# New places for the first query tile's attention among the main products, and an earlier load of x's first rows

## The chip, the cores and the metric

The kernel runs on one core of one Trainium2 chip. The metric is the device time of one execution in microseconds, taken as the median of three runs: 1147.26 us (1147.25 to 1148.64). The profiled execution took 1147.47 us, of which 1145.7 us lie between its first and its last instruction.

## The reference

Two layers of a decoder trunk work on x of 512 tokens by 1024 features, all in float32. Each layer is a mixer and then a gated MLP, both between root-mean-square norms. What matters here is the mixer's differential attention with 4 heads, each of which has two score maps and subtracts the second, weighted, from the first:

```
proj = rms_norm(x, g) @ w_in                     # 1024 -> 2560 columns
for query block i of 128 rows, head h:
    s = q[h, 0:2] @ k[h, 0:2].T * scale          # causal: keys of the blocks 0..i
    p = softmax(s)
    a = p[0] - lam * p[1]
    o[h] = a @ v[h]                              # 128 x 128
o = rms_norm(o, subln_g) * (1 - lam_init)        # a norm over each head's 128 columns
mix = concat(o, retention, pooling) @ w_out
x = x + rms_norm(mix, g2);  then the MLP: up projection, short convolution, gelu gate, down projection
```

There are four query blocks (i = 0 to 3). The first one has 128 keys only.

## The kernel before, in words

**Main products.** Nearly all of the time goes into four large products of each layer: the input projection (five strips of 512 columns: s = 0 for q, 1 for k, 2 for v, 3 for retention's q, k, v, 4 for gates and pooling), the output projection, the MLP's up projection and its down projection. Each operand is split into a high and a low part, so that one product of a 128-row slice takes three matmuls (`mm3`, line 489). Weights come through SyncE's DMA queue into one of three `raw` buffers (`emit_dma`, line 261) and are split by ScalarE (line 300) and VectorE (line 301) into `wa` and `wb` (`emit_split`, line 270).

**The planner.** While Python emits the program it counts main products in `now`: 512 columns of one matmul are one unit. After each `mm3` it calls `serve` (line 366) with three more units. The small steps of the mixer are generators (`scores`, `turns`, `values`, `outputs`, lines 886 to 915), each of which yields the place of its next step, in units from the layer's start, and the names of the steps that must have been emitted before. `serve` emits the step with the smallest place among those that are due and whose needs are done, until none is left. Places come from the table `PLACE` (line 45); a place is thus a due time, rounded up to the next multiple of three. `in_order` (line 332) ties every TensorE instruction behind the one emitted before it, so TensorE runs exactly in the planner's order, and if an instruction waits, everything behind it waits too. The order on VectorE and ScalarE is chosen by the framework from priorities; the planner's steps are emitted `ahead` of the main products' own work.

The planner counts 96 units for each of the five strips of the input projection. The four generators of attention are registered once strip 1 is emitted (line 977), at 192 units, and attention of the first query tile runs beside strip 2.

**The steps of one query tile i.** For each head h:

- `unit_a(h, i, m)` (line 720), m = 0 and 1: two score matmuls into a bank of role "s". There are two such banks, used in turn. VectorE adds the mask (line 730) and takes the maximum (line 731), ScalarE takes the exponential (line 733) and reads its row sum. After m = 1 VectorE forms the difference of the two maps (lines 738 to 740).
- `unit_b(h, i)` (line 742): TensorE turns the probabilities, ScalarE copies them out (line 749).
- `unit_c(h, i)` (line 752): TensorE multiplies them with v into the bank "o", 128 columns for each head. After the last head (h = 3) follows the norm: four squares with row sums on ScalarE (line 766), an addition (line 767), a reciprocal root of ten small VectorE instructions (lines 394 to 402), and one product of 512 columns (line 770) that leaves the normed tile in SBUF.
- `unit_e(i)` (line 781), once for each query tile: TensorE turns the four heads of the normed tile; it needs line 770's result. The result is split into the output projection's operand (lines 778 and 779).

Needs that matter: the scores of the fourth head need the first head's turning (`(l, "b", n - 3)`, line 889); a turning needs the values of two heads before it (line 897).

**The opening.** Before layer 0, x transposed (`xt`, four parts of 512 KB, each with two of the eight 128-feature slices) goes through two buffers into the split operand `ht` (`load_xt`, `split_xt`, lines 535 and 539); a third part waits until a buffer has been split. x itself (four tiles of 128 rows, `load_x`, line 567) is loaded as well, since the rows' norm factors (`row_factors`, line 447) come from it. They are squares on ScalarE (line 451) and a reciprocal root on VectorE. The factors are needed when the first strip's results leave PSUM (line 642). All of these transfers, the constants, the parameters and the four lambda vectors (line 249) are issued from SyncE's queue, in the order in which the code stands in lines 555 to 588. ScalarE's exponential for lambda is line 255.

Of the kernel before, what the change touches and what calls it, by code (L numbers as in the profile page):

```python
# [54 lines left out]
    ],  # L55
    "b": [[234, 235, 232, 242], [275, 278, 280, 287], [326, 334, 338, 320], [381, 385, 388, 418]],
    "c": [[241, 236, 242, 243], [282, 260, 284, 296], [330, 342, 326, 350], [386, 402, 397, 427]],
    "e": [264, 317, 373, 452],
    "rows": 404,
    "r1": [395, 431, 465, 513],  # L60
# [77 lines left out]
def tile_trunk(ctx: ExitStack, tc: tile.TileContext, x, xt, win, wout, wup, wdown, gpost, par, lam, const, out):  # L138
# [44 lines left out]
    def t4():  # L183
        return t4p.tile([P, D], F32, tag="t4", name=nm("t4"))
# [85 lines left out]
    def emit_split():  # L270

        j = state["split"]
        if j >= NU:
            return False
        kind, l, i = units[j][1]
        if i >= LAST3.get(kind, NFF):
            if not state["space"]:
                return False
            h, lo = state["space"].pop(0)
        else:  # L280
            if state["free"] == 0:
                return False
            state["free"] -= 1
            k = state["slot"] = (state["slot"] + 1) % NW
            h, lo = (wp.tile([P, D], F32R, tag=f"w{n}{k}", name=nm("w" + n)) for n in "ab")
        state["split"] += 1
        r = raws.pop(j)
        if kind == "down":
            se.copy(h, r)  # L289
            ve.tensor_tensor(out=lo, in0=r, in1=h.bitcast(F32), op=ALU.subtract)  # L290
        else:
            pr = params[l]
            if kind == "out":
                cuts = [(h, lo, r, pr["ws"][:, i:i + 1])]
            else:

                g = pr["gmix" if kind == "in" else "gmlp"]
                cuts = [(x[:, 0:512], x[:, 512:D], r[:, c * 512:(c + 1) * 512], g[:, 2 * i + c:2 * i + c + 1]) for c, x in enumerate((h, lo))]
            for a, b, x, sc in cuts:
                se.activation(a, x, AF.Copy, scale=sc)  # L300
                low = ve.scalar_tensor_tensor(b, x, sc, a.bitcast(F32), op0=ALU.mult, op1=ALU.subtract)  # L301
                if j == 0:
                    after(low, 0)
        halves[j] = [h, lo] if kind in LAST3 else [(x[:, 0:512], x[:, 512:D]) for x in (h, lo)]
        emit_dma()
        return True
# [228 lines left out]
    def load_xt(j):  # L535
        xparts[j] = t4()
        sy.dma_start(xparts[j], xt[j])

    def split_xt(j):
        r = xparts.pop(j)  # L540
        for c in range(2):
            dh = hth[:, 2 * j + c, :]
            if j or c:
                se.copy(dh, r[:, c * S:(c + 1) * S])
            else:
                opened.append(ve.tensor_copy(dh, r[:, c * S:(c + 1) * S]))
            low = ve.tensor_tensor(out=htl[:, 2 * j + c, :], in0=r[:, c * S:(c + 1) * S], in1=dh.bitcast(F32), op=ALU.subtract)
            if not (j or c):
                opened.append(low)
# [17 lines left out]
    def load_x(t):  # L567
        sy.dma_start(xs[:, t, :], x[t * P:(t + 1) * P, :])
        done.add((0, "xT", t))

    split_xt(0)
    emit_split()
    load_xt(2)
    split_xt(1)
    load_xt(3)
    load_x(0)
    emit_split()
    sy.dma_start(cst[:, 0:NCONST], const)
    derive_params(0)
# [618 lines left out]
```

## Time and profile before

| what | us |
|---|---|
| median of three runs | 1147.26 |
| the profiled execution | 1147.47 |
| its span, first to last instruction | 1145.7 |
| TensorE matmuls busy | 1133.6 (99%) |
| TensorE weight loads busy | 944.3 (82%) |
| VectorE busy | 738.8 (64%) |
| ScalarE busy | 548.1 (48%) |
| GpSimd busy | 11.9 (1%) |

Matmuls are pipelined in the records: a matmul of 512 columns is shown as busy for 0.39 us, while in a dense stretch the next one starts 0.23 us later. So the busy share of TensorE doesn't tell what is lost; one reads the distances between the starts. A row such as "L338 PE MATMUL ps_m<-wa,ht ... x3" is three matmuls in a row that write the tile ps_m from wa and ht. In the mixer ps_m is a main product of the strips 1 to 4, ps_s a score, ps_b a turning, ps_o the values. PE is TensorE, ACT ScalarE, DVE VectorE, SPq the queue of SyncE.

### The profile page before, as it was taken

To read this page: it belongs to the slowest core of one execution; us is meant where nothing else is said; L and a number is where in the kernel's file an instruction comes from. 1 tells how busy PE (TensorE), PEld (TensorE's weight loads), DVE (VectorE), ACT (ScalarE), POOL (GpSimd) and SP (SyncE) were. 2 spreads that over 40 slices of the span, in tenths; PEclk is the share of its full clock that TensorE was granted. 3 is DMA by queue.
4 is the path that set the end of the run, shared out by engine and by line. 5 is a ranking of instruction groups with operands and counts; after the bars stand their busy time and mean duration, and the time that the engine had idled before them with its cause. 6 is when DMAs were issued, how large, how long until landed. Compare 5 with 4: busy or idle time off the path is not lost.

```text
span 1145.7 us, 14829 instructions
## 1 busy us (share of the span) xinstructions
PE 1133.6 (99%) x5474; PEld 944.3 (82%) x5474; DVE 738.8 (64%) x1667; ACT 548.1 (48%) x1051; POOL 11.9 (1%) x20
## 2 busy tenths in 40 slices
PE   9999999999999999999999999999999999999997
PEld 6788878988888888888888888789888888888886
DVE  6988696777556457423777896876856655663224
ACT  6965543565444345312367754454645434452221
POOL 1000000000000000000000000000000000000000
PEclk9999999999999999999999999999999999999999
DMA  8411131332222232224023111313323232323211
GB/s 326 137 65 57 57 114 39 111 129 92 105 98 85 100 107 95 101 92 147 1 96 125 56 54 53 114 38 114 125 97 106 79 107 100 103 76 109 95 50 58
DMA packets 31320, 109.22 MB, mean 95 GB/s; under 512 B 3728, under 2 KB 4240, under 8 KB 31248
## 3 DMA queue, kind: packets, MB, share of 16 engines
q1 hardware_dynamic: 29808, 105.11, 26.5%
q10 hardware_dynamic: 1440, 3.17, 0.8%
q8 instruction: 43, 0.70, 0.2%
q14 instruction: 29, 0.24, 0.1%
HBM read 106.16 MB, written 2.10 MB: 94 GB/s over the span
## 4 chain that ended last, share of the span: by engine, by line
PE 91%; DVE 4%; ACT 2%; DMA 2%; issue 1%; SPq 0%; DVEq 0%; ACTq 0%
PE ps L338 72%; PE ps_m L338 11%; PE ps_b L341 2%; PE ps_b L338 2%; PE ps_o L338 2%; PE ps_s L338 1%; PE ps L341 1%; DMA rt<-in_lam 1%; DMA raw<-in_wout 1%; DVE ks L670 1%; DMA raw<-in_win 1%; ACT wa L300 0%; ACT t L733 0%; DVE space L301 0%; DVE wb L301 0%
## 5 line engine op out<-in xcount | busy, mean ns | idle before, releaser
L338 PE MATMUL ps<-ht,wb 128*128 128x512 f32 (+1 forms) x1176 | 305.0, 368 | 0.0
L338 PE MATMUL ps<-ht,wa 128*128 128x512 f32 (+1 forms) x1176 | 304.8, 367 | 0.0
L338 PEld LDWEIGHTS ps<-ht,wa 128*128 128x128 f32 x1176 | 210.3, 189 | 36.5
L338 PEld LDWEIGHTS ps<-ht,wb 128*128 128x128 f32 x1176 | 210.1, 188 | 36.5
L301 DVE SCALAR_TENSOR_TENSOR wa<-raw,par,wa 128x512 fp32r<-128x512 f32 x128 | 95.8, 749 | 143.5 <-ACT wa L300 143.2
L300 ACT ACTIVATE wa<-raw,par 128x512 fp32r<-128x512 f32 x128 | 92.2, 721 | 185.6 <-PE ps L338 173.4
L338 PE MATMUL ps<-wa,c 128*128 128x512 f32 x448 | 126.3, 394 | 0.0
L290 DVE TENSOR_TENSOR wb<-raw,wa 128x1024 fp32r<-128x1024 f32 x38 | 46.5, 1225 | 82.1 <-ACT wa L289 82.1
L301 DVE SCALAR_TENSOR_TENSOR wb<-raw,par,wb 128x512 fp32r<-128x512 f32 x128 | 95.8, 748 | 4.3 <-ACT wb L300 4.2
L338 PEld LDWEIGHTS ps<-wa,c 128*128 128x128 f32 x448 | 83.7, 188 | 18.0 <-issue 1.0
L338 PE MATMUL ps<-wa,ht 128*128 128x512 f32 x352 | 97.8, 391 | 0.3 <-DVE wa L301 0.3
L300 ACT ACTIVATE wb<-raw,par 128x512 fp32r<-128x512 f32 x128 | 91.9, 719 | 4.3 <-PE ps L338 3.2
L338 PE MATMUL ps_m<-wa,ht 128*128 128x512 f32 x288 | 83.6, 398 | 1.8 <-ACT t L642 1.8
L338 PE MATMUL ps_m<-wb,ht 128*128 128x512 f32 x288 | 83.2, 397 | 0.0
L289 ACT CAST wa<-raw 128x1024 fp32r<-128x1024 f32 x38 | 39.9, 1051 | 86.7 <-PE ps L338 86.7
L1068 ACT ACTIVATE t<-ps,par 128x512 f32<-128x512 f32 x88 | 67.5, 774 | 24.9 <-PE ps L338 24.9
L338 PEld LDWEIGHTS ps<-wa,ht 128*128 128x128 f32 x352 | 65.7, 188 | 14.3 <-DVE wa L301 0.6
L1069 DVE SCALAR_TENSOR_TENSOR t<-ps,par,t 128x511 f32<-128x511 f32 x88 | 65.2, 745 | 11.8 <-ACT t L1068 11.7
L338 PE MATMUL ps<-wb,c 128*128 128x512 f32 x224 | 71.8, 397 | 0.0
L338 PE MATMUL ps<-wb,ht 128*128 128x512 f32 x224 | 66.3, 389 | 0.0
L1070 DVE SCALAR_TENSOR_TENSOR t<-ps,par,t 128x510 f32<-128x510 f32 x88 | 65.1, 745 | 1.3
L338 PEld LDWEIGHTS ps_m<-wb,ht 128*128 128x128 f32 x288 | 52.5, 188 | 10.1
(194 smaller groups left out, 1416.5 us busy)
## 6 DMA issues: line engine op xcount, KB each, us to landing
raw<-in_wup SPq DMA_DIRECT2D x88, 512.0 KB, 3.5
raw<-in_wdown SPq DMA_DIRECT2D x44, 512.0 KB, 3.5
raw<-in_win SPq DMA_DIRECT2D x39, 512.0 KB, 3.6
raw<-in_wout SPq DMA_DIRECT2D x16, 512.0 KB, 3.5
xs<-in_x SPq DMA_DIRECT2D x4, 512.0 KB, 9.7
gain<-in_gpost ACTq DMA_DIRECT2D x4, 512.0 KB, 4.3
t<-in_xt SPq DMA_DIRECT2D x3, 512.0 KB, 5.6
out<-xs SPq DMA_DIRECT2D x4, 256.0 KB, 2.0
```

Source lines behind the costliest of these rows:

```text
L289: se.copy(h, r)
L290: ve.tensor_tensor(out=lo, in0=r, in1=h.bitcast(F32), op=ALU.subtract)
L300: se.activation(a, x, AF.Copy, scale=sc)
L301: low = ve.scalar_tensor_tensor(b, x, sc, a.bitcast(F32), op0=ALU.mult, op1=ALU.subtract)
L338: in_order(te.matmul(out, lhsT=lhsT, rhs=rhs, **k))
L341: in_order(te.transpose(out, in_, ident))
L670: ve.tensor_tensor(out=ks[o, :, m, sl], in0=bv[r], in1=ks[r, :, m, sl].bitcast(F32), op=ALU.subtract)
L1068: se.activation(acc, ps, AF.Identity, bias=conv[:, f, 3:4], scale=conv[:, f, 2:3])
L1069: ve.scalar_tensor_tensor(acc[:, 1:S], ps[:, 0:S - 1], conv[:, f, 1:2], acc[:, 1:S], op0=ALU.mult, op1=ALU.add)
L1070: ve.scalar_tensor_tensor(acc[:, 2:S], ps[:, 0:S - 2], conv[:, f, 0:1], acc[:, 2:S], op0=ALU.mult, op1=ALU.add)
```

## The change

Nine places in `PLACE` are new: in row i = 0 of "a" those of the first and of the last head, and the rows i = 0 of "b" and "c". The place of `unit_e(0)`, 264, stays. In the opening, `load_x(0)` moves from behind `load_xt(3)` to ahead of `split_xt(1)`, so that it stands before `load_xt(3)` in SyncE's queue. Both layers use the same table.

```diff
     "a": [
-        [[152, 202], [208, 214], [221, 225], [191, 214]],
+        [[192, 202], [208, 214], [221, 225], [227, 231]],
         [[240, 240], [250, 224], [262, 241], [270, 272]],
...
-    "b": [[234, 235, 232, 242], [275, 278, 280, 287], [326, 334, 338, 320], [381, 385, 388, 418]],
-    "c": [[241, 236, 242, 243], [282, 260, 284, 296], [330, 342, 326, 350], [386, 402, 397, 427]],
+    "b": [[228, 232, 241, 246], [275, 278, 280, 287], [326, 334, 338, 320], [381, 385, 388, 418]],
+    "c": [[238, 243, 250, 256], [282, 260, 284, 296], [330, 342, 326, 350], [386, 402, 397, 427]],
     "e": [264, 317, 373, 452],
...
     load_xt(2)
+    load_x(0)
     split_xt(1)
     load_xt(3)
-    load_x(0)
     emit_split()
     sy.dma_start(cst[:, 0:NCONST], const)
```

## Prediction

> **What bounds the kernel now.** I read the page first. TensorE is busy for all but 12 us of the span, so only what moves TensorE's own starts can move the end.
>
> ```profile
> span 1145.7 us, 14829 instructions
> PE 1133.6 (99%) x5474; PEld 944.3 (82%) x5474; DVE 738.8 (64%) x1667; ACT 548.1 (48%) x1051; POOL 11.9 (1%) x20
> ```
>
> Next, the list of waits, TensorE alone (total, times, longest). These three are its longest, and all lie in layer 0's opening; the rows behind them are shorter still:
>
> ```profile
> PE ps_m L338 <- ACT t L642: 1.8, 1, 1.8
> PE ps_o L338 <- DVE t L527: 1.2, 1, 1.2
> PE ps_b L341 <- ACT wb L300: 0.9, 1, 0.9
> ```
>
> So there is little to win. Third, the timeline of TensorE in layer 0, around the first query tile (start, duration, tile, count; ps_m are main products, ps_b turnings, ps_s scores, ps_o values):
>
> ```profile
> 66.71 0.85 PE L338 MATMUL ps_m<-wa,ht 128*128 128x512 f32 x3
> 67.40 0.86 PE L338 MATMUL ps_m<-wb,ht 128*128 128x512 f32 x3
> 68.09 0.27 PE L341 MATMUL ps_b<-cst,t 128*128 128x128 f32 x1
> 68.12 0.60 PE L338 MATMUL ps_s<-ks,c 128*128 128x256 f32 x3
> 68.56 0.28 PE L338 MATMUL ps_s<-ks,ql 128*128 128x256 f32 x1
> 68.67 0.86 PE L338 MATMUL ps_m<-wa,ht 128*128 128x512 f32 x3
> 69.37 0.27 PE L341 MATMUL ps_b<-cst,t 128*128 128x128 f32 x1
> 69.40 0.95 PE L338 MATMUL ps_m<-wb,ht 128*128 128x512 f32 x3
> 70.48 0.73 PE L338 MATMUL ps_s<-ks,c 128*128 128x256 f32 x3
> ...
> 72.42 0.27 PE L341 MATMUL ps_b<-cst,t 128*128 128x128 f32 x1
> 72.83 0.76 PE L338 MATMUL ps_o<-vv,t 128*128 128x128 f32 x4
> 73.34 0.94 PE L338 MATMUL ps_m<-wb,ht 128*128 128x512 f32 x3
> ...
> 78.72 0.52 PE L338 MATMUL ps_s<-ks,c 128*128 128x256 f32 x3
> 79.08 0.28 PE L338 MATMUL ps_s<-ks,ql 128*128 128x256 f32 x1
> 79.37 0.66 PE L341 MATMUL ps_b<-cst,t 128*128 128x128 f32 x4
> ```
>
> Read the starts. Three main products take 0.69 us (66.71 to 67.40): that is one slot of the planner, three units. The turning at 68.09 is the one with place 234, so the three starting at 66.71, 67.40 and 68.67 bring the count to 231, 234 and 237, and so on. The order in the trace is the planner's: at 234 the first turning and the fourth head's two scores, at 237 the second turning, at 240 two scores of tile 1, at 243 (up to 73.34) a clump of four values and two turnings, at 264 two scores and then `unit_e(0)` at 79.37. Three waits lie in it: 0.30 us before 70.48 (69.40 plus 0.78, what three products take behind a turning, would be 70.18), 0.38 us before 72.83 (a turning is otherwise followed 0.03 us later, as at 68.09), and 0.18 us before 79.37 (the last score takes 0.11, as at 68.56). Together 0.86 us. The same clump in layer 1 loses about the same.
>
> **The change part by part.**
>
> *What does not move.* The generators are registered at 192 units, so a first score with place 152 ran at the first call after that, 195; with 192 it runs there too. The next five scores keep their places. Cost nothing, by the code.
>
> *The fourth head's scores come earlier.* They need the first turning, now at 228 (66.71 above); they follow it there (place 227) and at 231. In their way is a bank: the two banks are used in turn, and the first of these scores takes the bank of the third head's first map, which ScalarE reads last here:
>
> ```profile
> 67.65 0.19 ACT L733 ACTIVATION_READ_ACCUMULATOR t<-ps_s,sm 128x1 f32 x1
> ```
>
> That ends at 67.84, and nothing before it is moved. TensorE arrives at 66.74 and waits about 1.1 us; before, it came at 68.12, when the bank was free. The main products queue behind the score. Bounds: nothing, if ScalarE's and VectorE's work for these maps is put earlier, and 1.4 us, the whole advance (66.74 to 68.12). I take 1.1, since nothing of that work has a new place.
>
> *The clump is spread.* The values run at 240, 243, 252, 258, the turnings at 228, 234, 243, 246: never a turning and its value in one slot, so ScalarE's copy between them is hidden by at least two slots, and the scores of tile 1 at 240 come a whole slot behind the fourth head's. The 0.30 and 0.38 us go. The matmuls are the same ones; I count nothing for their new neighbours.
>
> *What comes late next.* The last value moves from 243 to 258, but `unit_e(0)` stays at 264, and it needs the norm behind the last value. TensorE can't pass it: all later instructions are queued behind the four turnings. The norm, on ScalarE and VectorE:
>
> ```profile
> 73.62 0.28 ACT L766 ACTIVATE t<-ps_o 128x128 f32<-128x128 f32 x1
> ```
>
> ```profile
> 74.80 0.16 DVE L767 TENSOR_TENSOR sm<-sm,sm 128x4 f32<-128x4 f32 x1 [0.32 <-ACT t L766]
> 75.00 0.17 DVE L394 TENSOR_SCALAR sm<-sm 128x4 int32<-128x4 int32 x1
> ...
> 78.62 0.69 DVE L770 TENSOR_TENSOR t<-ps_o,sm 128x512 f32<-128x512 f32 x1
> ```
>
> From the end of the values (73.34) to the turnings (79.37) this took 6.03 us, and before it was covered by seven slots, 243 to 264, but for the 0.18 us. Now two slots and two scores remain: 0.78 + 0.69 + 0.47 (78.72 to 79.08 and 0.11) = 1.94 us. So the wait is the chain less 1.94. How long is the chain? Three prices. Without any neighbour: 1.46 to line 767 (73.34 to 74.80), eleven small steps of 0.20 (as from 74.80 to 75.00), 0.69 for line 770 and 0.06 to TensorE: 4.41. As it was in tile 0, with two weight splits and a score's mask and maximum among the small steps: 6.03. And as in tile 1, with the masks and maxima alone:
>
> ```profile
> 90.87 0.61 PE L338 MATMUL ps_o<-vv,t 128*128 128x128 f32 x4
> ```
>
> ```profile
> 95.74 0.69 DVE L770 TENSOR_TENSOR t<-ps_o,sm 128x512 f32<-128x512 f32 x1
> ```
>
> These end near 91.2 as the next start sees them (0.61 busy less the last one's 0.27 of pipeline), and line 770 ends at 96.43: about 5.3 with the step to TensorE. In the new place the chain meets tile 1's next scores (they stand right before `unit_e(0)`) and part of a weight split, so I take 5.6, between the two: a wait of **3.7 us**, with ends at 2.5 and 4.1. The old wait of 0.18 is replaced by it.
>
> Per layer: +1.1 - 0.30 - 0.38 - 0.18 + 3.7 = +3.9. A check from the other end: the fourth head's first score at 67.84, then ten slots to 258 (6.9 to 7.0), and in between six scores (two took 0.55 from 68.12 to 68.67), four values (two heads' took 0.51 from 72.83 to 73.34, each in two matmul records) and three turnings of 0.03, together some 2.7: the last value ends near 77.5, and 77.5 + 5.6 = 83.1 against 79.37 is +3.7. I take **+3.8 for each layer**. Layer 1 has the same order and the same wait:
>
> ```profile
> 639.34 0.75 PE L338 MATMUL ps_o<-vv,t 128*128 128x128 f32 x4
> ...
> 645.87 0.66 PE L341 MATMUL ps_b<-cst,t 128*128 128x128 f32 x4
> ```
>
> The end of its values is 0.51 behind 639.34 as in layer 0, so the chain took 6.02. Two layers: +7.6. No later wait gives it back: the list has none that could shrink in return.
>
> *The clock.* A wait of 3.7 us is longer than any TensorE has here, and the granted clock (next to last three columns: PEclk, DMA, GB/s) reacts to idling:
>
> ```profile
> 30.00:32.00 2.00, 0.56 (x3) 0.13 (x1) 1.90 (x6) 1.95 (x4) 0.00 (x0) 1.00 0.75 242
> 1140.00:1142.00 2.00, 0.00 (x0) 0.00 (x0) 1.89 (x6) 0.20 (x1) 0.00 (x0) 0.89 0.00 0
> ```
>
> The idle 1.8 us around 31 left it at 1.00. After the last matmuls it fell within the second of these windows: a mean of 0.89 of 1.00 and, if the lower value is one half, a fall 0.45 us before 1142, at 1141.5.
>
> ```profile
> 1136.74 2.20 PE L338 MATMUL ps<-space,c 128*128 128x512 f32 x9
> ```
>
> These nine end at 1138.94, so 2.6 us of idling were enough there. What it costs shows in the opening:
>
> ```profile
> 1.18 4.16 PE L338 MATMUL ps_o<-t 128*128 128x512 bf16 x10 [1.18 <-DVE t L527]
> ```
>
> The first ten matmuls of 512 columns take about 0.42 us each (4.16 over ten), against 0.23 in the dense rows above, for some 3.8 us without the pipeline of the last. So a halving behind the wait costs between nothing (if it ends within the wait) and half of 3.8, 1.9 us. I take 1.0 for each layer: **+2.0**. The Trainium skill, "TensorE: Matmul & The Clock Gate", Part 1, says the same from the other side: the gate looks at free-running windows of about 3.4 us, an idle one halves the clock and a busy one restores it, and it advises against idle gaps over about 3 us between matmuls. By that rule a gap of 3.7 us costs up to 1.7 us, an estimate; the trace agrees in both directions, with 2.6 us to the fall and 3.8 us to the rise.
>
> *x's first rows.* One transfer of 512 KB changes places with another on SyncE's queue: the last quarter of xt, which waits there for a buffer, now stands behind x's rows, which wait for nothing. What follows, lambda's vector included, keeps its turn. The quarter lands later. Its casts are the two here, and ScalarE was idle until it landed:
>
> ```profile
> 16.03 1.15 ACT L544 CAST ht<-t 128x512 fp32r<-128x512 f32 x2 [1.42 <-DMA t<-in_xt]
> ```
>
> TensorE has no wait there now; I bound the loss by as much again, +1.4. The gain could come at lambda's exponential, which stands ahead of the squares of x's rows and waits for its vector:
>
> ```profile
> 22.84 0.20 ACT L255 ACTIVATE sm<-sm 128x2 f32<-128x2 f32 x1 [2.95 <-DVE sm L253]
> 22.95 0.62 ACT L451 ACTIVATE t<-xs 128x512 f32<-128x512 f32 x1
> ```
>
> The squares give the rows' factors for line 642, on which TensorE's 1.8 us hang. If earlier rows let the squares go ahead into such idle time, this wait and the 0.9 us of the same list can vanish: -2.7. I take -0.3, near to nothing, since ScalarE's order is the framework's choice and no row shows another one.
>
> **Sum.** 7.6 + 2.0 - 0.3 = +9.3 on the profiled execution's 1147.47 (span 1145.7 and 1.8 around it): 1156.8. The median of the runs lies 0.2 lower: **1156.6 us**.
>
> **The rivals.**
>
> *No halving.* The two waits come, but the clock stays up through one or both: 7.6 - 0.3, so 1154.6 with both. For it: 1.8 us of idling left the clock alone, and the trace has a single fall, at the end, where nothing follows. Against: 2.6 us sufficed for that one. Chance 0.3; with the shortest chain, 2.5 us, it is 1152.2.
>
> *Nothing to measure.* Places are due times, and needs may hold the steps where they were: 1147.3. For it: the unmoved first scores. Against: turnings and values need only what is done by 225. With a wait of half the size and the full gain of the opening it comes to the same. Chance 0.06.
>
> *Faster.* One mechanism: the squares of x's first rows go ahead of lambda's exponential, and the opening gives 2.7 us. With 0.86 per layer from the clump and the bank free in time that is -4.4, 1142.9. It decides only if the norm stays hidden: two waits of 2.2 us each would eat it, that is a chain over 4.1 us, and the shortest price above is 4.41. Chance 0.04.
>
> The forecast has 0.60. A measurement of this kernel can tell about 0.2%, 2.3 us, from no change. Slower by more than that: 0.6 + 0.3 = 0.90; within: 0.06; faster: 0.04. The range: below, the shortest waits (7.6 - 2.4 = 5.2), no halving and the opening's full gain, +2.5, 1149.8; above, waits of 4.1, halvings of 1.9: 8.4 + 3.8 = +12.2, 1159.5; that the opening loses its 1.4 on top of both is left out.
>
> **What would show it.** In the profile after: TensorE's list of waits has a row of 7 us in two for ps_b, released by VectorE's line 770; the timeline shows two slots between the last values and the four turnings; a wait of about 1 us for ps_s, released by line 733; none at the old 70.48 and 72.83. The granted clock dips behind each long wait. In the opening the squares (line 451) either still follow the exponential (line 255), with the wait for line 642 unchanged, or precede it. I am wrong if the turnings of `unit_e(0)` aren't late: if the chain takes under 3 us or the planner put more slots in between.

## The result, and the profile after

The changed kernel takes 1161.41 us (median of 4 runs, 1160.5 to 1161.91) against 1147.43 us (1147.25 to 1148.64): a ratio of 1.0117, 95% interval 1.0105 to 1.0129. It is slower, as forecast, but by 14.0 us and not by 9.3, and 1161.41 lies above the range's upper end of 1159.5. Its profiled execution took 1161.33 us.

The page's head shows TensorE with almost the same busy time as before (1137.0 against 1133.6 us) in a span that is 13.8 us longer:

```profile
span 1159.5 us, 14831 instructions
PE 1137.0 (98%) x5474; PEld 947.7 (82%) x5474; DVE 739.6 (64%) x1667; ACT 548.3 (47%) x1051; POOL 11.9 (1%) x20
```

The head of the list of TensorE's waits of the changed kernel (total, times, longest):

```profile
PE ps_b L341 <- DVE t L770: 10.0, 2, 5.1
PE ps_s L338 <- ACT t L733: 2.1, 2, 1.1
PE ps_m L338 <- ACT t L642: 1.8, 1, 1.8
```

The first two rows are new, and are the forecast ones: the turnings of `unit_e(0)` behind the norm, and the fourth head's score behind the read of its bank. Of the opening's three waits, the 0.9 us for ps_b is gone and the 1.8 us for line 642 is not. The timeline of TensorE, at the fourth head's first score (first two rows) and from the last values to `unit_e(0)`:

```profile
65.87 0.27 PE L341 MATMUL ps_b<-cst,t 128*128 128x128 f32 x1
67.07 0.50 PE L338 MATMUL ps_s<-ks,c 128*128 128x256 f32 x2 [0.93 <-ACT t L733]
...
76.52 0.38 PE L338 MATMUL ps_o<-vv,t 128*128 128x128 f32 x2
76.66 0.95 PE L338 MATMUL ps_m<-wa,ht 128*128 128x512 f32 x3
77.44 0.85 PE L338 MATMUL ps_m<-wb,ht 128*128 128x512 f32 x3
78.13 0.52 PE L338 MATMUL ps_s<-ks,c 128*128 128x256 f32 x3
78.49 0.28 PE L338 MATMUL ps_s<-ks,ql 128*128 128x256 f32 x1
83.63 1.11 PE L341 MATMUL ps_b<-cst,t 128*128 128x128 f32 x4 [4.86 <-DVE t L770]
84.40 1.63 PE L338 MATMUL ps_m<-wa,ht 128*128 128x512 f32 x3
85.83 1.48 PE L338 MATMUL ps_m<-wb,ht 128*128 128x512 f32 x3
...
88.35 0.85 PE L338 MATMUL ps_m<-wb,ht 128*128 128x512 f32 x3
```

Between the values and the turnings stand exactly the two slots and two scores of the prediction, and by starts the turnings wait 5.03 us (78.49 plus 0.11 to 83.63). Behind them the distance of three main products is 1.43 us (84.40 to 85.83) where it was 0.69: the clock is halved. The windows view says so in its third column from the end (before it are the window, its length, and busy time and count of PE, PEld, DVE, ACT, POOL; behind it DMA and GB/s):

```profile
80.00:82.00 2.00, 0.00 (x0) 0.00 (x0) 2.00 (x9) 0.60 (x4) 0.00 (x0) 0.87 0.03 12
82.00:84.00 2.00, 0.37 (x2) 0.37 (x3) 1.44 (x6) 0.00 (x0) 0.00 (x0) 0.50 0.72 217
...
88.00:90.00 2.00, 2.00 (x13) 1.73 (x12) 0.69 (x2) 1.45 (x3) 0.00 (x0) 0.93 0.00 0
```

Halved from 81.47 to 88.30, the trace's clock records say: 6.83 us, of which the last 4.7 lie over work. Where the 13.9 us of the two profiled executions lie, read from TensorE's starts:

| start of | before | after | later | in this stretch |
|---|---|---|---|---|
| the first score, layer 0 | 56.52 | 55.70 | -0.82 | -0.82 opening |
| `unit_e(0)`'s turnings, layer 0 | 79.37 | 83.63 | +4.26 | +5.08 waits |
| the first score, layer 1 | 623.00 | 629.55 | +6.55 | +2.29 halved clock |
| `unit_e(0)`'s turnings, layer 1 | 645.87 | 657.77 | +11.90 | +5.35 waits |
| the last matmul | 1138.55 | 1152.42 | +13.87 | +1.97 halved clock |

### The profile page after: what moved, and what is told of

The parts are those of the page before. It is cut to its first block, busy times and chain, and to the rows that moved or that the text cites. A ratio compares the mean times of both kernels' runs of the same rounds, so it can differ in the third digit from the quotient of the medians.

```text
span 1159.5 us, 14831 instructions
## 1 busy us (share of the span) xinstructions
PE 1137.0 (98%) x5474; PEld 947.7 (82%) x5474; DVE 739.6 (64%) x1667; ACT 548.3 (47%) x1051; POOL 11.9 (1%) x20
## 4 chain that ended last, share of the span: by engine, by line
PE 93%; DVE 3%; ACT 2%; DMA 1%; issue 1%; DVEq 0%; ACTq 0%
PE ps L338 73%; PE ps_m L338 12%; PE ps_o L338 2%; PE ps_b L341 2%; PE ps_b L338 2%; PE ps_s L338 2%; PE ps L341 1%; DMA raw<-in_wout 1%; DVE ks L670 1%; DVE wb L301 0%; DVE space L301 0%; ACT t L733 0%; ACT wa L300 0%; ACT ks L669 0%; ACT t L642 0%
## 5 line engine op out<-in xcount | busy, mean ns | idle before, releaser
L338 PE MATMUL ps_m<-wa,ht 128*128 128x512 f32 x288 | 86.3, 408 | 1.8 <-ACT t L642 1.8
L338 PEld LDWEIGHTS ps<-wa,ht 128*128 128x128 f32 x352 | 66.3, 189 | 13.9 <-issue 0.3
```

The lines of the kernel that those rows point to most:

```text
L338: in_order(te.matmul(out, lhsT=lhsT, rhs=rhs, **k))
```

## The experiments

The theory after the result: one wait for each layer, behind a norm that takes longer in its new place than the first tile's did before, and a clock that is halved for two whole periods by each wait. Its rivals: the main products' order or the opening lose the time; the norm's length is its own and not its neighbours'; the time behind the wait is something other than the clock. All medians below are beside runs of the kernel before on the same chip.

**The two halves alone.** Before with only `load_x(0)` moved, and before with only the table.

> Only the load of x's first rows is moved; the table is the old one. Late-norm theory: the opening's part of the change is a gain of 0.8 us (the first score starts at 55.70 in the changed kernel and at 56.52 before), so about 1146.6, and the first score is again near 55.7. Rival, the opening: the late last quarter costs time and is part of the loss of 14 us; then this kernel is slower than before by 0.5 us or more.

Measured: 1146.76 us against 1147.8, ratio 0.9991 (0.9982 to 1.0). The 0.9 us for ps_b is gone, the 1.8 us stays.

> Only the table is changed; the opening is the old one. Late-norm theory: the whole loss and the opening's 0.8 us beside it, 1147.4 + 14.8 = 1162.2, with both long waits for the normed tile (5.0 and 5.3 us) and both halvings. Rival, the opening: clearly less than the changed kernel's 1161.4.

Measured: 1162.56 us against 1147.8, ratio 1.0122 (1.0107 to 1.0136). The halves add up: the table costs all of it, and the opening gives about 1 us back (0.8 by the profiles; the interval of e1 just reaches 1).

**Is it the wait?** The changed kernel, with `unit_e(0)` six slots later:

```diff
-    "e": [264, 317, 373, 452],
+    "e": [282, 317, 373, 452],
```

> The changed kernel with the place of the first query tile's output turnings at 282 in place of 264, eight slots behind the last values. Late-norm theory: both long waits go to under 0.5 us, so do the halvings (granted clock back at 0.998); what is left is the opening's -0.8, the clump's -0.6 to -0.7 for each layer and the bank wait's +1.2 and +1.4: 1147.4 + 0.5, 1147 to 1149. Rival, the spread itself: the loss comes from the other moved places, and 5 us or more of it stays, over 1152.

Measured: 1149.35 us against 1147.8, ratio 1.0011 (1.0003 to 1.002). One number of the table takes 12 of the 14 us away. In its profile the waits for the normed tile's turnings and the halvings are gone (mean clock 0.999 against 0.993). Three rows of its list of waits are left over from the table:

```profile
PE ps_s L338 <- ACT t L733: 2.1, 2, 1.2
...
PE ps_o L338 <- DVE t L770: 1.0, 1, 1.0
PE ps_o L338 <- ACT vv L673: 0.7, 1, 0.7
```

The first is the bank of the fourth head's score. The other two are new and stand before tile 1's first value, one in each layer: it needs the bank "o", which line 770 reads, and starts 0.15 us behind that line's end in both layers. In layer 0 the list puts the wait down to line 673, which forms v and ends there 0.14 us behind line 770.

Two places between the two:

```diff
-    "e": [264, 317, 373, 452],
+    "e": [270, 317, 373, 452],
```

> The changed kernel with the output turnings' place at 270 in place of 264: two slots (1.4 us) more between the last values and them. Late-norm theory: the waits shrink by 1.4 each, to 3.6 and 3.9 us, which is still long enough for the halved clock: 1161.4 - 2.8 = 1158.6, 1157 to 1160, with granted clock under 0.997. Rival, wait and clock as one smooth cost: the halved clock shrinks in proportion as well, 1157.4 or less.

Measured: 1158.17 us against 1147.35, ratio 1.0093 (1.0075 to 1.0111). The norm takes 6.98 us in both layers, and each of the two waits is 1.5 to 1.6 us shorter by the list (7.0 in two), while the clock is still halved behind both. The four runs lie from 1156.2 to 1160.62, and their mean clocks from 0.997 down to 0.991: how many periods are halved differs between executions, so that this run can't tell the theory from the rival of one smooth cost.

```diff
-    "e": [264, 317, 373, 452],
+    "e": [276, 317, 373, 452],
```

> The changed kernel with the output turnings' place at 276: four slots, two scores and a turning more (3.5 us), so waits of 1.5 and 1.8 us. Late-norm theory: no wait is long enough for a halving, granted clock 0.998 or more, 1161.4 - 7.0 - 4.3 = 1150.1. Rival, smooth cost: 1161.4 - 7.0 - 3.0 = 1151.4 with a dip of the clock behind each wait.

Measured: 1155.67 us against 1147.35, ratio 1.0074 (1.006 to 1.0088), 5.6 us more than expected. The slots bought half of the 11.3 us that were expected, for two reasons. The norm went from 6.97 to 7.82 us (values' end to turnings), because the slots let a third instruction of line 301 (the weight splits) and two more masks in among its small steps; so 2.3 us of waiting were left. And these sufficed for the clock:

```profile
86.21 0.66 PE L341 MATMUL ps_b<-cst,t 128*128 128x128 f32 x4 [2.27 <-DVE t L770]
...
87.91 1.63 PE L338 MATMUL ps_m<-wb,ht 128*128 128x512 f32 x3
```

The wait had been over for 0.9 us when the halving set in (87.11 in the clock records), and the products at 87.91 run slowly. It is not the idling itself that runs slowly, but the work of a later period.

**Is it the clock?** The changed kernel, with 18 idle products of 512 columns into the turnings' own bank, emitted ahead of `unit_e(0)`'s turnings, so that TensorE has work while it waits:

```diff
+            for _ in range(18 if i == 0 else 0):
+                mm(b, lhsT=hth[:, 0, 0:P], rhs=hth[:, 0, :], start=True, stop=True)
```

> The changed kernel with 18 idle products of 512 columns put on TensorE ahead of the first query tile's output turnings, into the bank that the turnings then overwrite (4.1 us at full clock, inside the wait of 5.0 to 5.3). They compute nothing that is used. If the halved clock is a cost of its own (2.3 and 2.0 us by the starts in the changed kernel), it goes and the wait's end stays: 1161.4 - 4.3 = 1157.1, granted clock 0.998 in all. Rival, the wait alone: the time stays at 1161.4 or rises.

Measured: 1157.04 us against 1147.8, ratio 1.0082 (1.0065 to 1.0099). Its timeline:

```profile
78.37 4.26 PE L338 MATMUL ps_b<-ht 128*128 128x512 f32 x18
83.39 0.66 PE L341 MATMUL ps_b<-cst,t 128*128 128x128 f32 x4 [0.76 <-DVE t L770]
83.81 0.94 PE L338 MATMUL ps_m<-wa,ht 128*128 128x512 f32 x3
...
85.28 0.85 PE L338 MATMUL ps_m<-wa,ht 128*128 128x512 f32 x3
85.96 0.39 PE L338 MATMUL ps_m<-wb,ht 128*128 128x512 f32 x1
```

The norm takes as long as in the changed kernel (6.97 and 7.25 us), so the turnings are as late. But the four turnings and nine products take 2.57 us (83.39 to 85.96) where the changed kernel needed 4.72 (83.63 to 88.35). So 2.15 us is what the halving costs in layer 0; over both layers the two medians differ by 4.4 us. The mean clock of the profile is 0.998, and no halving lies in it before the last matmul. Nothing but the filler differs, so that the time behind the waits is the clock is shown.

**Is the norm's length its neighbours'?** The changed kernel, with tile 1's scores, which stand right ahead of `unit_e(0)`, behind it:

```diff
-        [[240, 240], [250, 224], [262, 241], [270, 272]],
+        [[240, 240], [250, 224], [265, 241], [270, 272]],
```

> The changed kernel with the place of two scores of tile 1 at 265 in place of 262, so that they stand behind the output turnings and their masks and maxima no longer among the norm's small steps. Why was the norm 6.9 to 7.2 us long where 5.6 was forecast? If VectorE's queue is the reason (the scores' mask ahead of line 767, then masks, maxima and two weight splits in between), it shortens by about 1.5 us, to 5.4; the turnings are reached 0.47 earlier, so waits of about 4 us: 1161.4 - 2.1 = 1159.3. Rival: the norm is slow for another reason (contention, slower steps): it stays at 6.9, and the time at 1161.4 or above.

Measured: 1158.98 us against 1147.35, ratio 1.0103 (1.0089 to 1.0117). The norm takes 5.64 us in layer 0. VectorE's timeline shows what is left among its steps, the two instructions of a weight split:

```profile
77.93 0.16 DVE L767 TENSOR_TENSOR sm<-sm,sm 128x4 f32<-128x4 f32 x1
...
78.61 0.75 DVE L301 SCALAR_TENSOR_TENSOR wa<-raw,par,wa 128x512 fp32r<-128x512 f32 x1
...
79.35 0.74 DVE L301 SCALAR_TENSOR_TENSOR wb<-raw,par,wb 128x512 fp32r<-128x512 f32 x1
...
81.18 0.69 DVE L770 TENSOR_TENSOR t<-ps_o,sm 128x512 f32<-128x512 f32 x1
```

**The bank alone.** Before, with the fourth head's scores and the first turning at the new places:

```diff
-        [[152, 202], [208, 214], [221, 225], [191, 214]],
+        [[152, 202], [208, 214], [221, 225], [227, 231]],
-    "b": [[234, 235, 232, 242], ...
+    "b": [[228, 235, 232, 242], ...
```

> The old kernel, in which the fourth head's scores go to 227 and 231 and the first turning to 228; values, other turnings, outputs and the opening stay. It prices the bank wait by itself: +1.2 in layer 0 and +1.4 in layer 1 for it, less the 0.3 to 0.4 of the old wait of tile 1's scores in each layer, so +1.8 us, 1149.5. Rival: the bank's wait is hidden, since the scores of tile 1 and all behind them gain what it costs; then 1147.8 as before.

Measured: 1150.07 us against 1147.35, ratio 1.0025 (1.0014 to 1.0036). Its list of waits has the bank's 2.1 us in two, as the changed kernel has it, and 1.2 us of a value's wait for line 749 beside it. So the earlier scores cost by themselves. That it is 2.7 us and not the 1.8 that were expected has two reasons in the profile: the value's wait, and a halved period in the opening (last section), in which the bank has no part.

**Can the spread table win?** With the fourth head's scores back at 234 and 237, the clump spread, tile 1's first scores a slot later, `unit_e(0)` late, and the moved load:

```diff
-        [[152, 202], [208, 214], [221, 225], [191, 214]],
-        [[240, 240], ...
+        [[192, 202], [208, 214], [221, 225], [234, 237]],
+        [[243, 243], ...
...
-    "b": [[234, 235, 232, 242], ...
-    "c": [[241, 236, 242, 243], ...
-    "e": [264, 317, 373, 452],
+    "b": [[228, 231, 240, 246], ...
+    "c": [[237, 240, 246, 250], ...
+    "e": [279, 317, 373, 452],
```

> The changed kernel with a table drawn from what the runs showed: first turnings at 228 and 231, the fourth head's scores at 234 and 237 (when their banks are free), values at 237, 240, 246, 250, the other turnings at 240 and 246, tile 1's first scores at 243, and the output turnings at 279, nine slots behind the last values and ahead of tile 1's values. Late-norm theory: no long wait, no bank wait, no clump, and the opening's gain stays: 1147.4 - 0.8 - 0.9 for each layer = 1144.8, at most 1146. Rival, the spread itself costs: 1147.4 or more.

Measured: 1151.02 us against 1147.64, ratio 1.003 (1.0019 to 1.004), 6 us more than expected. Two rows of its list of waits:

```profile
PE ps_s L338 <- ACT t L733: 2.9, 4, 1.1
PE ps_b L341 <- DVE ks L670: 1.8, 2, 1.0
```

No wait for the norm, but two that I had not priced: the second turning's bank is still read by k's split (line 670), and tile 1's scores meet banks that VectorE serves late, since the norm (7.4 us here) and they share its queue. Together they are 4.7 of the 6 us.

**The opening's own wait.** Before with the moved load, and seven idle products into a spare bank where TensorE waits 1.8 us for line 642:

```diff
+                if l == 0 and s == 1 and n == 1:
+                    spare = bank("o")
+                    for _ in range(7):
+                        mm(spare, lhsT=hth[:, 0, 0:P], rhs=hth[:, 0, :], start=True, stop=True)
```

> The old table with the moved load (e1) and seven idle products of 512 columns into a spare bank ahead of the strip-1 product that waits 1.8 us in the opening (1.6 us, inside that wait; nothing uses what they compute). Several runs with that wait show a halved clock for 3.4 us at 32 us, others don't. If the wait's place in the gate's window decides, filling it takes the slower times away: all runs between 1146 and 1147, granted clock 0.999. Rival: the spread of about 2 us between executions has another cause and stays.

Measured: 1146.48 us against 1147.64, ratio 0.9992 (0.9983 to 1.0001). The filler costs nothing, since it stands in a wait (1.8 us has become 0.2). Its 11 runs lie from 1146.02 to 1147.38, the 23 of before from 1146.36 to 1149.13: the interval just reaches 1, while the longer runs are absent. The moved load alone doesn't take them away: e1's 11 runs, on another chip, lie from 1146.24 to 1148.49.

> Both: the table of e9 and the filled opening wait. Late-norm theory: e9's time, 1144.8, without executions that are 1.5 us longer. Rival: as in e9 and e10.

Measured: 1150.63 us against 1147.64, ratio 1.0021 (1.0012 to 1.0031). The new table with the filler, no better than without it.

Last, the version with the filler and a smaller step: tile 1's scores at 243, the third head's values moved to 246 and the fourth's with them, `unit_e(0)` at 267:

```diff
-        [[240, 240], ...
+        [[243, 243], ...
...
-    "c": [[241, 236, 242, 243], ...
-    "e": [264, 317, 373, 452],
+    "c": [[241, 236, 246, 246], ...
+    "e": [267, 317, 373, 452],
```

> e10 with the two waits of the clump taken out by one slot each: tile 1's first two scores at 243 in place of 240, the last two heads' values at 246 in place of 242 and 243, the output turnings at 267 in place of 264, so that their distance stays. Every step moves backward, none ahead of its buffer. Late-norm theory: the norm stays at about 6.0 us and fits, 0.30 and 0.38 us of waits and the slow scores of 0.2 go in each layer: 1146.5 - 1.6 = 1144.9. Rival: the norm grows with its new neighbours, or the scores behind meet their banks, and the gain is lost: 1146.5 or more.

Measured: 1150.45 us against 1146.91, ratio 1.0027 (1.0017 to 1.0038), again above what was expected. ScalarE's timeline shows the norm's first square:

```profile
73.21 0.73 ACT L300 ACTIVATE wa<-raw,par 128x512 fp32r<-128x512 f32 x1 [0.15 <-PE ps_m L338]
73.84 0.26 ACT L766 ACTIVATE t<-ps_o 128x128 f32<-128x128 f32 x1
```

The values end at 72.23; before, the squares began 0.28 us behind them, here 1.61 us, behind tile 1's exponentials and a weight split. The norm takes 7.9 us, and the turnings wait 1.9 us in each layer. Its eight runs lie from 1148.64 at a mean clock of 0.999 to 1152.22 at 0.995. None of the tables I tried beats the one of before; the version with the moved load and the filler is level with it or a little ahead.

## Why the prediction was wrong in size

**Right: what moves and what comes late.** The three small waits of the old places are gone. The bank's wait is 1.17 us in layer 0 (65.87 plus 0.03 to 67.07), forecast 1.1. Two slots and two scores remain between the values and `unit_e(0)`, as counted, and the wait is the norm less 1.94 us: 6.97 - 1.94 = 5.03, which is what the starts show. Slower is the right side, and its cause is the one named; e3 takes it away and leaves 1.6 us above the kernel before.

**Wrong: the norm's length, 5.6 us.** It took 6.97 us in layer 0 and 7.23 in layer 1, above the upper end of 6.03. Term by term: 2 x 3.7 became 5.03 + 5.29, and that is 2.9 of the 4.6 us by which the sum is short. The step that failed is "the chain meets tile 1's next scores [...] and part of a weight split, so I take 5.6, between the two". I took the longer of two old norms for the worst case, without listing the neighbours of the new place, and misread the old ones: the 6.03 us have two masks and two maxima among the small steps, not one of each. The old trace also has longer norms, at which the prediction didn't look. Tile 2's, from the end of its values (111.22) to the end of line 770, takes 6.41 us, and tile 3's 8.25 (139.55 to 147.80). Tile 2's, with longer rows (512 keys), shows in the kernel before much of the arrangement that was to come: the next scores right behind the values, their masks ahead of line 767, and line 740 among the steps:

```profile
111.22 0.95 PE L338 MATMUL ps_s<-ks,c 128*128 128x512 f32 x3
```

```profile
112.43 0.30 DVE L730 TENSOR_TENSOR ps_s<-ps_s,cst 128x128 f32<-128x128 f32 x1 [0.17 <-PE ps_s L338]
112.67 0.16 DVE L767 TENSOR_TENSOR sm<-sm,sm 128x4 f32<-128x4 f32 x1
...
116.28 0.75 DVE L740 SCALAR_TENSOR_TENSOR t<-t,sm,t 128x512 f32<-128x512 f32 x1
116.95 0.68 DVE L770 TENSOR_TENSOR t<-ps_o,sm 128x512 f32<-128x512 f32 x1
```

VectorE's timeline of the changed kernel:

```profile
78.57 0.30 DVE L730 TENSOR_TENSOR ps_s<-ps_s,cst 128x128 f32<-128x128 f32 x1 [0.36 <-PE ps_s L338]
78.78 0.15 DVE L767 TENSOR_TENSOR sm<-sm,sm 128x4 f32<-128x4 f32 x1
78.85 0.29 DVE L730 TENSOR_TENSOR ps_s<-ps_s,cst 128x128 f32<-128x128 f32 x1
...
79.12 0.42 DVE L731 TENSOR_REDUCE sm<-ps_s 128x1 f32<-128x256 f32 x1
...
79.93 0.75 DVE L301 SCALAR_TENSOR_TENSOR wa<-raw,par,wa 128x512 fp32r<-128x512 f32 x1
...
80.74 0.73 DVE L301 SCALAR_TENSOR_TENSOR wb<-raw,par,wb 128x512 fp32r<-128x512 f32 x1
...
81.71 0.48 DVE L740 SCALAR_TENSOR_TENSOR t<-t,sm,t 128x256 f32<-128x256 f32 x1
...
82.88 0.69 DVE L770 TENSOR_TENSOR t<-ps_o,sm 128x512 f32<-128x512 f32 x1
```

Line 767 starts 2.12 us behind the values' end (76.66), 1.46 before. Of these 0.66 us, 0.17 are ScalarE's: it begins the squares 0.47 us behind the values, after an exponential of tile 1, and not 0.28, so that they end at 78.26. The other 0.49 are VectorE's: line 767 stands behind a mask that itself waits for tile 1's next scores, which TensorE reaches two slots behind the values, and not three as before. From line 767 to line 770 it is 4.10 us against 3.82, with one mask less and the difference of the two maps (lines 738 to 740) as new neighbours. Together 0.94, the whole growth; the small steps themselves take 0.15 to 0.17 us each in both. With tile 1's scores behind `unit_e(0)` (e8) line 767 starts 1.64 us behind the values and the norm takes 5.64 us. That this is near the 5.6 that I took is chance, since the prediction described the place with those scores. With more slots in between (e6) it grew to 7.82. So the norm's length belongs to its place; a number carried over from another place was a guess within too narrow bounds.

**Wrong: the halving's price, 1.0 us for each layer.** It cost 2.15 in layer 0 and 1.85 in layer 1 (there 3.47 us for turnings and six products against 1.87 in e4, and half of the 0.49 us until the clock came back), 2.0 more than forecast in all. The step that failed is "half of 3.8, 1.9 us" as the most: it took the opening's stretch for the length of any halving. The last section shows why it lasts longer.

**The opening** was forecast at -0.3 and gave -0.82. ScalarE's order did not change, and line 451 still follows line 255:

```profile
22.02 0.20 ACT L255 ACTIVATE sm<-sm 128x2 f32<-128x2 f32 x1 [2.61 <-DVE sm L253]
22.13 0.61 ACT L451 ACTIVATE t<-xs 128x512 f32<-128x512 f32 x1
```

Both come 0.82 us earlier, and with them all that follows; 0.9 us is what the one vanished wait cost. Lambda's transfer, which the prediction left in its turn at no gain, was issued 0.34 us earlier (13.27 and not 13.61) and landed 8.1 us later, not 8.6, so that its first use (line 251) starts at 21.38 and not at 22.19. Why the transfer itself was shorter wasn't tried.

**The rivals.** *No halving* had 0.3 and fell: both waits halved the clock, and the mean clock is 0.993 in all four runs. Its argument, that 1.8 us of idling left the clock at 1.00, doesn't hold in every execution (below). *Nothing to measure* and *faster* fell with the first row of the list of waits.

## What to carry to other kernels

When a step is moved towards its consumer, don't carry the length of its chain over: list whose instructions stand next to it in its new place on each engine's queue, and price the chain with all of them, and with those that wait themselves. An engine whose order is written out pays for a late result at once, so leave slots for the longest chain, and see whether more slots draw more neighbours in. If TensorE has to wait, count its work by the clock's periods: a wait can cost more behind it than its own last microseconds, and idle products put into it cost nothing here (e4, e10).

## What the runs showed of the hardware

**The clock changes on a grid.** In the changed kernel the clock records have changes at 6.376, 81.469 and 88.296: 22 and 24 steps of 3.413 us behind the first. In the kernel before, 4.910 and 1141.548 lie 333 such steps apart. So a halving lasts whole periods, one or two here. By the busy time of TensorE in each period (as the profile models it), changed kernel, the period with the wait and the two behind it:

```profile
78.06:81.47 3.41, 0.71 (x6) 0.46 (x4) 3.04 (x15) 2.46 (x8) 0.00 (x0) 1.00 0.47 154
81.47:84.88 3.41, 1.25 (x5) 1.25 (x6) 1.97 (x9) 0.10 (x1) 0.00 (x0) 0.50 0.49 154
84.88:88.30 3.42, 3.42 (x9) 2.64 (x8) 0.69 (x1) 0.49 (x1) 0.00 (x0) 0.50 0.00 0
```

A period with 0.71 of 3.41 us busy halved the next one; that one, with 1.25 busy, didn't bring the clock back; a full one did. In e5, 2.05 busy didn't bring it back either, and 2.92 did. Had the wait ended a little earlier, in the first period, one period would have been lost and not two: e6 is that case, with 1.14 busy in the one before and one halved period.

**How little idling is enough** depends on where it falls. The kernel before, the period with its 1.8 us wait:

```profile
28.80:32.22 3.42, 1.76 (x10) 1.17 (x8) 3.29 (x13) 3.14 (x8) 0.00 (x0) 1.00 0.48 157
32.22:35.63 3.41, 3.29 (x14) 2.74 (x15) 3.40 (x10) 3.41 (x8) 0.00 (x0) 1.00 0.06 17
```

and in e7, the same wait of the same kernel's opening, at another phase of the grid:

```profile
29.49:32.90 3.41, 1.64 (x7) 1.24 (x7) 3.30 (x13) 3.36 (x7) 0.00 (x0) 1.00 0.38 144
32.90:36.31 3.41, 3.41 (x9) 2.63 (x8) 3.37 (x10) 3.32 (x8) 0.00 (x0) 0.50 0.50 144
```

1.76 busy left the clock alone, 1.64 halved it, and so did 1.48 in e12 (a wait of 1.93 us); two periods of e12 with 2.41 and 2.49, over which a like wait is spread, did not. So the edge lies near half a period, but this busy time doesn't decide the single case: the same opening wait, with 1.64 busy, halved the clock in e5 and e6 as well, and with 1.63 in e8 and 1.64 in e4 it did not; nor did 1.53 in e1, in the period in which the last matmul ends. The Trainium skill, "TensorE: Matmul & The Clock Gate", Part 1, has the free-running window of 3413 ns, and the trace agrees; its advice in the section "Why this matters for your kernels", no idle gaps over about 3 us, is too generous for this case, where 1.8 to 2.3 us halved the clock when most of it fell into one window. The 2.6 us to the fall at the end of the kernel before, which the prediction counted as agreement, are under 3 us too.

The opening's wait may so halve the clock in some executions of the kernel before, and make its runs differ by some 2 us. The profiles of e5, e6 and e7 show that halving, and the filler's narrower spread (e10) fits it. The runs' mean clocks fit it too: one halved period takes 0.0015 off the mean, and the fall behind the last matmul took 0.0006 to 0.0020 in the profiles, so that 0.997 or less needs, by this estimate, a halved period elsewhere. Of the 67 runs of the kernel before beside the experiments, on three chips, the 15 with 0.997 or less took 1147.63 to 1149.39 us, and the 20 with 0.999 took 1146.21 to 1148.21. But no profile of the kernel before caught the halving itself: for that kernel it is argued, not shown.
